# Summing most of a modulation matvec on VectorE instead of TensorE in a hybrid GLA / SSD / PEER block

## The chip, the cores and the metric

One core of one Trainium2 chip runs the kernel. The metric is device time in microseconds, from a run without the profiler; the kernel before was timed three times. One further execution was recorded by the profiler, and all rows below come from that one.

## The reference

One layer over 256 latent tokens with a prefix of 256 context tokens, D = 2048, all float32. Cut to what matters here:

```python
mod_x = jnp.split((silu(c)     @ w_ada + b_ada)[:, None, :],    6, axis=-1)   # w_ada: 2048 x 12288
mod_c = jnp.split((silu(c_ctx) @ w_ada + b_ada)[None, None, :], 6, axis=-1)
hc = rmsnorm(ctx, norm1_w) * (1 + mod_c[1]) + mod_c[0]
hx = rmsnorm(x, norm1_w)   * (1 + mod_x[1]) + mod_x[0]
core_c, ctx_states = branch_core(hc, 1, p, None)        # h @ w_in, GLA and SSD scans
core_x, _          = branch_core(hx, rows, p, ctx_states)
x   = x + mod_x[2] * branch_out(core_x, p)
hx2 = rmsnorm(x, norm2_w) * (1 + mod_x[4]) + mod_x[3]
x   = x + mod_x[5] * peer(hx2, peer_wq, peer_keys, peer_u, peer_v)
return rmsnorm(x, final_norm_w)
```

The change is about the first two lines: a row vector of 2048 numbers times a weight of 96 MB (2048 x 12288 float32), for two vectors, `c` and `c_ctx`. Parts one and two (columns 0 to 4095) are needed for both vectors before anything else can start. Parts three to six are needed later, and with one layer only for `c`.

## The kernel before, in words

Every big weight passes through the class `Stream`: a plan lists 512 KB chunks of 128 x 1024 float32 in the order of use, `_load` (line 39) issues the DMA of a chunk on SP's queue, and `_split` (line 47) turns a float32 chunk into two reduced-precision halves, `hi` with a copy on ScalarE (line 52) and `lo` with a subtraction on VectorE (line 53). A product is then three matmuls per k-tile, hi x hi, hi x lo, lo x hi (`mm3`, lines 314 to 316; `v_part`, lines 322 to 324). `ahead()` keeps loads 7 chunks and splits 3 chunks ahead of use; 4 buffers hold raw chunks and 4 each hold `hi` and `lo`.

The order on each engine is the order in which the Python code issues the instructions. Every engine executes its own list in that order, and SP's list holds the weight loads.

The program goes through these stages.

- **The start.** The tokens `xc` (4 MB) are loaded, `norm1` (lines 279 to 294) squares them on ScalarE (line 284), adds on VectorE (286), sums over partitions on TensorE (287), takes the reciprocal root (289, 290) and multiplies (293). In parallel `ada_piece` (line 248) computes parts one and two of the modulation: `w_ada` chunks of 4 k-tiles x 256 columns, each as four plain float32 matmuls that put a k-tile each into one of four 32-column strips of the array (line 253, `cS` stationary). After four chunks `ada_out` (line 256) copies the partial sums to SBUF (259), transposes them on TensorE (264) and sums them on VectorE (270, 271). The list `START` (line 139) fixes how chunks of the modulation, the modulated tokens `h_pair` (298 to 307) and the first projections are interleaved: each of its ten rounds uses two k-tiles of the first `v` projection and of the small `ld` projection; rounds 0 to 7 also take eight modulation chunks each, and four rounds take one `k` tile.
- **The projections**, with the GLA and SSD scans as generators in the background. `ftile` calls `tick()` after each chunk (lines 895 to 898), and `tick` (342) lets every background generator go one step. Every second tick it calls `ride_piece` (349): one chunk of parts three to six, 2 k-tiles x 512 columns, again four float32 matmuls on line 253. There are 120 such chunks; their loads lie in the same plan, one after every two weight chunks.
- **The output projections** (`oproj`, lines 1044 to 1074), then `w_o` (1101 to 1121). The last 8 modulation chunks were loaded by POOL's queue into `fill` and are multiplied at line 1122, while the second norm is computed.
- **PEER**: queries, routing, then the products with `u` and `v` (lines 1308 to 1479).

```python
def tick(riding=True):
    step()
    ticks += 1
    if riding and ticks % RIDE == 0 and ride_n < 128 - FILL:
        ride_piece()
```

Of the kernel before, what the change touches and what calls it, by code (L numbers as in the profile page):

```python
# [10 lines left out]
F32 = mybir.dt.float32  # L11
# [17 lines left out]
class Stream:  # L29
# [3 lines left out]
    def __init__(self, nc, pool, loads, splits):  # L33
        self.nc, self.pool, self.loads, self.splits = nc, pool, loads, splits
        self.plan, self.raw, self.done = [], {}, {}
        self.cur = self.nd = self.ns = 0
        self.limit = self.side = None

    def _load(self, i):
# [4 lines left out]
        self.nc.sync.dma_start(t, self.plan[i][0])  # L44
        self.raw[i] = t

    def _split(self, i):
        t = self.raw.pop(i)
        if self.plan[i][1]:
            hi = self.pool.tile([P, 1024], F32R, name="hi", tag="hi", bufs=self.splits + 1)  # L50
            lo = self.pool.tile([P, 1024], F32R, name="lo", tag="lo", bufs=self.splits + 1)
            self.nc.scalar.activation(hi, t, AF.Copy)  # L52
            self.nc.vector.tensor_sub(lo, t, hi.bitcast(F32))  # L53
            self.done[i] = (hi, lo)
        else:
            self.done[i] = t
# [25 lines left out]
def hybrid_block_kernel(ctx, tc, A, out):  # L82
# [8 lines left out]
    st = Stream(nc, streams, 7, 3)  # L91
# [13 lines left out]
    def f_chunks(arr, f):  # L105
        return [(arr[f, h], True) for h in range(arr.shape[1])]
# [5 lines left out]
    RIDE, FILL = 2, 8  # L112
# [10 lines left out]
    def v_chunks(hd, q):  # L123
        return [(A["w_v"][hd, 2 * q + i], True) for i in range(2)]

    def unit_chunks(u):
        k, a, b = u
        first, n = {"k": (K0 + 2 * a + b, 1), "q": (Q0 + 2 * a, 2), "r": (R0 + 4 * a, 4), "xs": (X0 + 4 * a + b, 1),
                    "B": (B0 + a, 1), "C": (C0 + a, 1), "z": (Z0 + 4 * a + 2 * b, 2), "gl": (G0 + 2 * a, 2),
                    "v": (0, 0)}[k]  # L130
        if k == "v":
            return sum((v_chunks(a, q) for q in range(4)), [])
        if k == "k" and a < 2:
            return [(W[first, 1], True)]
        return sum((f_chunks(W, first + i) for i in range(n)), [])
# [16 lines left out]
    plan = []  # L152
    for k, a, b in START:
        if k == "ada":
            plan.append((A["w_ada0"][a, b], False))
        elif k == "v" and b == 0:
            plan.append((A["w_v"][0, a], True))
        elif k == "ld" and b == 0 and a % 2 == 0:
            plan.append((A["w_ld"][a // 2], True))
        elif k == "k":  # L160
            plan.append((W[K0 + a, 0], True))
    st.limit = len(plan)
    ride = [(A["w_ada1"][b, i], False) for b in range(16) for i in range(8)]
    nt = 0
    for u in units:
        for c in unit_chunks(u):
            plan.append(c)
            nt += 1
            if nt % RIDE == 0 and len(ride) > FILL:
                plan.append(ride.pop(0))  # L170
    assert len(ride) == FILL
# [6 lines left out]
    last_ada = ride  # L178
    QORD = [(j, e, h) for h in range(2) for j in range(2) for e in range(2)]
    QORD += [(j, e, h) for j in range(2, 8) for e in range(2) for h in range(2)]  # L180
    plan += [(A["w_q"][2 * j + e, h], True) for j, e, h in QORD]
    NB = 32
    for b in range(NB + BACK):
        for i in range(4):
            if b < NB:
                plan += f_chunks(A["u"], 4 * b + i)
            if b >= BACK:
                plan += [(A["v"][b - BACK, 2 * i + j], True) for j in range(2)]
# [3 lines left out]
    xpool = ctx.enter_context(tc.tile_pool(name="hpool", bufs=1))  # L192
# [13 lines left out]
    st.side = (xp, 5)  # L206
# [4 lines left out]
    nc.vector.tensor_scalar(ident, jp, 0.0, None, op0=OP.is_equal)  # L211
    ones = consts.tile([P, P], F32, name="ones")
    nc.vector.memset(ones, 1.0)
    ones512 = consts.tile([P, 256], F32, name="ones512")
    nc.vector.memset(ones512, 1.0)
# [7 lines left out]
    selF = consts.tile([P, 2, P], U32, name="selF")  # L223
    selB = consts.tile([P, 2, P], U32, name="selB")
    for n in range(2):
        nc.vector.tensor_scalar(selF[:, n], jp, 0.0, None, op0=OP.is_ge)
        nc.vector.tensor_scalar(selB[:, n], jp, 0.0, None, op0=OP.is_le)
# [20 lines left out]
    def ada_piece(i, ps, halves, raw=None):  # L248

        raw = (st.get() if raw is None else raw).rearrange("p (g n) -> p g n", g=4)  # L250
        nk = 4 // halves
# [4 lines left out]
    def ada_out(b, ps, halves):  # L256

        sb = xpool.tile([P, 256], F32, name="adasb", tag="adasb", bufs=2)
        nc.scalar.activation(sb, ps, AF.Copy)
        yield  # L260
        yield
        p2 = scbank((P, 2, P))
        for t in range(2):
            nc.tensor.transpose(p2[:, t], sb[:, t * P:(t + 1) * P], ident)
        yield
        p2 = p2.rearrange("p t (j h m) -> p h t m j", h=halves, m=32)
        for h in range(halves):
            n = 2 * (halves * b + h)
            dst = mods[:, :, n:n + 2]
            nc.vector.tensor_reduce(dst.rearrange("p m t -> p t m"), p2[:, h, :, 0:2, :], axis=AX.X, op=OP.add)  # L270
            nc.vector.tensor_add(dst, dst, b_ada[:, None, n:n + 2].to_broadcast([P, 2, 2]))
        ended.add(("ada", b))
        yield
# [57 lines left out]
    ride_n, ride_ps = 0, None  # L331
# [17 lines left out]
    def ride_piece(raw=None):  # L349
        nonlocal ride_n, ride_ps  # L350
        b, i = divmod(ride_n, 8)
        if i == 0:
            ride_ps = adb[:, b % 2]
        ada_piece(i, ride_ps, 2, raw)
        if i == 7:
            bg.insert(0, ada_out(8 + b, ride_ps, 2))
        ride_n += 1

# [5 lines left out]
    adb = psum.tile([P, 2, 256], F32, name="ad")  # L364
    pv0 = [mmbank() for _ in range(4)]
    n1 = norm1()
    plr = pdt = None
    Kt = {a: w4.tile([P, 2, 512], F32, name="s4", tag="s4", bufs=5) for a in range(2)}
    for k, a, b in START:
        if k == "ada":  # L370
            if b == 0:
                ps = adb[:, a // 8]
            ada_piece(b, ps, 1)
            if b == 3:
                bg.append(ada_out(a, ps, 1))
# [28 lines left out]
    st.ahead()  # L404
    SZ = {"s1": 256, "s2": 512, "s4": 1024}
# [37 lines left out]
    def decay(hd):  # L443
# [10 lines left out]
        def one(d, k):  # L454
# [12 lines left out]
            for n in range(2):  # L467
                s = slice(n * P, n * P + P) if d == 0 else slice(n * P + P - 1, n * P - 1 if n else None, -1)
                nc.vector.tensor_tensor_scan(B[:, k, s], ones512[:, :P], mn[:, s], 0.0, op0=OP.mult, op1=OP.add)
# [4 lines left out]
            nc.vector.tensor_tensor_scan(B[:, k, o], ones512[:, :255], mn[:, s], 0.0, op0=OP.mult, op1=OP.add)  # L474
# [152 lines left out]
    def dt_stage(pd):  # L627
# [26 lines left out]
        for c in range(4):  # L654
            s = slice(c * P, c * P + P)
            r = slice(c * P + P - 1, c * P - 1 if c else None, -1)
            nc.vector.tensor_tensor_scan(cum[rows[0], s], ones512[rows[0], :P], dA[rows[0], s], 0.0, op0=OP.mult, op1=OP.add)
            nc.vector.tensor_tensor_scan(cum[rows[1], r], ones512[rows[1], :P], dA[rows[1], r], 0.0, op0=OP.mult, op1=OP.add)
# [419 lines left out]
    def wo_load(i):  # L1078

        if i < 8:  # L1080
            nc.gpsimd.dma_start(x1[:, 2 * i:2 * i + 2], A["xc"][:, 2 * i:2 * i + 2, 0:256])
            if i < FILL:
                fill.append(x1p.tile([P, 1024], F32, name="fill", tag="fill", bufs=FILL))
                nc.gpsimd.dma_start(fill[-1], last_ada[i][0])
# [37 lines left out]
    for t in fill:  # L1122
        ride_piece(t)
# [183 lines left out]

    pq = {}
# [174 lines left out]
def _layouts(I):  # L1483
# [6 lines left out]
    L["w_ada0"] = f(w[:, :2 * D].reshape(4, 4, P, 16, 256).transpose(3, 0, 2, 1, 4)).reshape(16, 4, P, 1024)  # L1490
    L["w_ada1"] = f(w[:, 2 * D:].reshape(8, 2, P, 16, 512).transpose(3, 0, 2, 1, 4)).reshape(16, 8, P, 1024)
# [52 lines left out]
```

## Time and profile before

| what | value |
|---|---|
| median of 3 runs | 3682.08 us (3681.17 to 3683.45) |
| the profiled execution | 3680.64 us, span 3678.8 us |
| TensorE matmul busy | 3619.1 us, 98% of the span |
| TensorE weight load busy | 3194.6 us, 87% |
| VectorE busy | 2227.3 us, 61% |
| ScalarE busy | 1669.3 us, 45% |
| GpSimd busy | 370.1 us, 10% |
| weight DMAs on SP's queue | 625.03 MB, 50.9% of 16 engines |

Busy time of TensorE is modelled: matmuls overlap in the array, and what one costs is read from the distance between the starts of its neighbours. The chain of waits follows the work that ended last back to the start of the program and says which engine held it. A wait in the list of waits is put down to what came last. A number of the profile is a line of the kernel before.

### The profile page before, as it was taken

Reading aid. Unit: us, or ns where it says so; the run is one execution under the profiler, and the core shown is the slowest. Engines: PE = TensorE matmul, PEld = TensorE weight load, DVE = VectorE, ACT = ScalarE, POOL = GpSimd, SP = SyncE. Lnnn points to the kernel's source line nnn. Section 1 sums busy time; section 2 is a strip of 40 time slices with the busy share of each in tenths; the row PEclk is TensorE's granted clock in tenths of the full one; section 3 lists DMA queues with packets and bytes.
Section 4 is the critical chain, followed back from the end, with each engine's and each line's share of the span. In section 5 each row is a group of like instructions: output and inputs, shape, how many; then the busy total and the mean of one; then the engine's idle time right before and its main releaser. Section 6 shows DMA issues by size and latency. Waiting matters only on the chain.

```text
span 3678.8 us, 60850 instructions
## 1 busy us (share of the span) xinstructions
PE 3619.1 (98%) x24799; PEld 3194.6 (87%) x24799; DVE 2227.3 (61%) x3405; ACT 1669.3 (45%) x2248; POOL 370.1 (10%) x424
## 2 busy tenths in 40 slices
PE   6999999999999999999999999999999999999998
PEld 3688888888888888899999999999999999998886
DVE  4364443565566566656555788785555555556777
ACT  3244443344544455555444445554444444444444
POOL 0000000000000000011002006362000000000004
PEclk9999999999999999999999999999999999999999
DMA  8564444546555564467657556677665666666764
GB/s 341 214 177 142 151 166 164 188 152 199 192 172 164 185 204 144 135 206 266 195 189 258 176 179 197 200 200 228 197 198 196 199 197 198 196 199 202 244 227 141
DMA packets 196873, 715.51 MB, mean 194 GB/s; under 512 B 22769, under 2 KB 22913, under 8 KB 196081
## 3 DMA queue, kind: packets, MB, share of 16 engines
q1 hardware_dynamic: 171648, 625.03, 50.9%
q0 software_dynamic: 24944, 86.59, 8.5%
q8 instruction: 195, 3.19, 0.4%
q14 instruction: 86, 0.70, 0.1%
HBM read 679.93 MB, written 31.60 MB: 193 GB/s over the span
## 4 chain that ended last, share of the span: by engine, by line
PE 94%; DVE 2%; DMA 1%; ACT 1%; issue 1%; SPq 0%; POOL 0%; DVEq 0%; ACTq 0%; POOLq 0%
PE mm L314 20%; PE mm L315 20%; PE mm L316 20%; PE mm L1459 6%; PE mm L1460 6%; PE mm L1461 6%; PE ad L253 2%; PE mm L322 2%; PE sc L838 2%; PE mm L323 2%; PE mm L324 2%; PE sc L1267 2%; DVE lo L53 1%; PE sc L579 1%; PE sc L771 1%
## 5 line engine op out<-in xcount | busy, mean ns | idle before, releaser
L53 DVE TENSOR_TENSOR lo<-raw,hi 128x1024 fp32r<-128x1024 f32 x996 | 1235.1, 1247 | 1044.2 <-ACT hi L52 1040.4
L52 ACT ACTIVATE hi<-raw 128x1024 fp32r<-128x1024 f32 x996 | 1048.2, 1058 | 1248.8 <-PE mm L315 549.6
L314 PE MATMUL mm<-Hhi,hi 128*128 128x256 f32 (+1 forms) x2272 | 741.9, 327 | 3.7 <-ACT hi L52 3.1
L316 PE MATMUL mm<-Hhi,lo 128*128 128x256 f32 (+1 forms) x2272 | 723.0, 318 | 2.5 <-DVE lo L53 2.5
L315 PE MATMUL mm<-Hlo,hi 128*128 128x256 f32 (+1 forms) x2272 | 722.1, 318 | 0.0
L314 PE MATMUL mm<-h2hi,hi 128*128 128x256 f32 x2304 | 656.9, 285 | 3.3 <-ACT h2hi L1135 3.3
L315 PE MATMUL mm<-h2lo,hi 128*128 128x256 f32 x2304 | 652.4, 283 | 0.2
L316 PE MATMUL mm<-h2hi,lo 128*128 128x256 f32 x2304 | 651.8, 283 | 0.0
L314 PEld LDWEIGHTS mm<-Hhi,hi 128*128 128x128 f32 x2272 | 433.0, 191 | 82.3 <-issue 45.8
L316 PEld LDWEIGHTS mm<-Hhi,lo 128*128 128x128 f32 x2272 | 433.5, 191 | 33.0 <-DVE lo L53 3.1
L315 PEld LDWEIGHTS mm<-Hlo,hi 128*128 128x128 f32 x2272 | 433.7, 191 | 28.0 <-issue 0.5
L314 PEld LDWEIGHTS mm<-h2hi,hi 128*128 128x128 f32 x2304 | 441.6, 192 | 7.0 <-ACT h2hi L1135 3.7
L315 PEld LDWEIGHTS mm<-h2lo,hi 128*128 128x128 f32 x2304 | 441.9, 192 | 3.9 <-DVE h2lo L1138 0.7
L316 PEld LDWEIGHTS mm<-h2hi,lo 128*128 128x128 f32 x2304 | 441.6, 192 | 0.0
L1460 PE MATMUL mm<-lo,ph 128*128 128x512 f32 x1024 | 405.6, 396 | 4.5 <-DVE lo L53 4.5
L1459 PE MATMUL mm<-hi,ph 128*128 128x512 f32 x1024 | 406.3, 397 | 0.0
L1461 PE MATMUL mm<-hi,pl 128*128 128x512 f32 x1024 | 404.9, 395 | 0.0
L1460 PEld LDWEIGHTS mm<-lo,ph 128*128 128x128 f32 x1024 | 192.7, 188 | 48.6 <-DVE lo L53 6.0
L1461 PEld LDWEIGHTS mm<-hi,pl 128*128 128x128 f32 x1024 | 192.7, 188 | 46.6
L1459 PEld LDWEIGHTS mm<-hi,ph 128*128 128x128 f32 x1024 | 193.0, 188 | 43.1
L698 DVE SCALAR_TENSOR_TENSOR s<-mm,convw,s 128x189 f32<-128x189 f32 (+2 forms) x384 | 160.1, 427 | 111.5 <-ACT s L690 107.5
L316 PE MATMUL mm<-yh,lo 128*128 128x256 f32 x768 | 217.5, 283 | 1.3 <-DVE lo L53 1.3
(328 smaller groups left out, 4518.1 us busy)
## 6 DMA issues: line engine op xcount, KB each, us to landing
raw<-in_w_f_dram SPq DMA_DIRECT2D x288, 512.0 KB, 3.7
raw<-in_u_dram SPq DMA_DIRECT2D x256, 512.0 KB, 3.5
raw<-in_v_dram SPq DMA_DIRECT2D x256, 512.0 KB, 4.2
raw<-in_w_ada_dram SPq DMA_DIRECT2D x184, 512.0 KB, 4.3
raw<-in_w_so_dram SPq DMA_DIRECT2D x64, 512.0 KB, 3.4
raw<-in_w_v_dram SPq DMA_DIRECT2D x32, 512.0 KB, 3.9
s<-cum_d POOLq DMA_DIRECT2D x64, 256.0 KB, 6.6
raw<-in_w_ga_dram SPq DMA_DIRECT2D x32, 512.0 KB, 4.8
```

The lines of the kernel that those rows point to most:

```text
L52: self.nc.scalar.activation(hi, t, AF.Copy)
L53: self.nc.vector.tensor_sub(lo, t, hi.bitcast(F32))
L253: mm_(ps[32 * g:32 * g + 32, :], cS[:, nk * i + g // halves, :], raw[:, g, :], start=i == 0, stop=i == KT // nk - 1, tile_position=(0, 32 ...
L314: mm_(ps, Whi[:, j, :], hi[:, k, tok], start=start and j == 0, stop=False)
L315: mm_(ps, Whi[:, j, :], lo[:, k, tok], start=False, stop=False)
L316: mm_(ps, Wlo[:, j, :], hi[:, k, tok], start=False, stop=stop and j == n - 1)
L322: mm_(pv[tb], Hhi[:, k, tok], Whi[:, j, :], start=k == 0, stop=False)
L323: mm_(pv[tb], Hhi[:, k, tok], Wlo[:, j, :], start=False, stop=False)
L698: nc.vector.scalar_tensor_tensor(dst, xi[:, r0 + dr:r1 + dr, c0 + dc:c1 + dc], w[:, t:t + 1], dst, op0=OP.mult, op1=OP.add)
L1459: mm_(ps[t, i], ghi, Whi, start=j == 0 and k == 0, stop=False)
L1460: mm_(ps[t, i], ghi, Wlo, start=False, stop=False)
L1461: mm_(ps[t, i], glo, Whi, start=False, stop=j == 1 and k == 1)
```

## The change: what it does, and the diff

Parts one and two stay on TensorE, and so do the last 512 columns of part six. Their chunks become pairs of 512 KB loads of 2 k-tiles x 512 columns; four matmuls of 512 columns replace four of 256, so the start has 32 pieces where there were 64, and eight `ada_out` where there were 16. Instead of a transpose, a product with a 0/1 matrix `sel2` brings a result over partitions.

The other 7680 columns of parts three to six, for `c` only, are cut into 15 blocks of 512 columns with 16 k-tiles each, 240 tiles of 128 x 512 (256 KB). At every tick `ride_piece` takes one such tile and VectorE multiplies it by the k-tile's 128 numbers (one per partition) and adds the previous sum: a `tensor_scalar` for the first k-tile of a block, a `scalar_tensor_tensor` for the other 15. After the sixteenth, `ride_out` sums over partitions with four matmuls on TensorE (the sums are stationary, one column of ones moves) and VectorE adds the bias.

These loads leave the plan. `board()` issues them on SP's queue, in the start up to 7 ahead into other pools, later up to 3 ahead into four 256 KB buffers. The weight stream keeps 6 chunks ahead instead of 7, with 3 raw buffers instead of 4. All of its entries are now split, so the first three chunks are split at the place of the first `ahead()`.

```diff
     def _load(self, i):
-        if self.side and not self.plan[i][1] and i % 3:
-            t = self.side[0].tile([P, 1024], F32, name="raw0", tag="raw0", bufs=self.side[1])
-        else:
-            t = self.pool.tile([P, 1024], F32, name="raw", tag="raw", bufs=self.loads - self.splits)
+        t = self.pool.tile([P, 1024], F32, name="raw", tag="raw", bufs=self.loads - self.splits)
...
+    def board(self):
+
+        n = 2 if self.side else 1
+        while self.nr < len(self.rides) and len(self.aboard) + n <= (7 if self.side else 3):
+            for _ in range(n):
+                if not self.side:
+                    t = self.pool.tile([P, 512], F32, name="ride", tag="ride", bufs=4)
+                elif self.nr % 7 > 1:
+                    t = self.side[0].tile([P, 1024], F32, name="raw0", tag="raw0", bufs=5)
+                else:
+                    t = self.side[1].tile([P, 1024], F32, name="s4", tag="s4", bufs=5)
+                self.nc.sync.dma_start(t, self.rides[self.nr])
+                self.aboard.append(t)
+                self.nr += 1
...
-    st = Stream(nc, streams, 7, 3)
+    st = Stream(nc, streams, 6, 3)
...
-    RIDE, FILL = 2, 8
+    FILL = 4
...
-            if c < 8:
-                START.append(("ada", (8 + c, c)[i // 4], i % 4))
+            if c < 8 and i % 2:
+                START.append(("ada", c, i // 2))
...
-    st.side = (xp, 5)
+    st.side = (xp, w4)
+    st.board()
     st.ahead()
...
-    def ada_piece(i, ps, halves, raw=None):
+    adb = psum.tile([P, 512], F32, name="ad")
+
+    def ada_piece(i, raws=None):
...
         for g in range(4):
-            mm_(ps[32 * g:32 * g + 32, :], cS[:, nk * i + g // halves, :], raw[:, g, :], start=i == 0, stop=i == KT // nk - 1,
+            mm_(adb[32 * g:32 * g + 32, :], cS[:, 4 * i + g, :], raws[g // 2][:, g % 2, :], start=i == 0, stop=i == 3,
                 tile_position=(0, 32 * g), skip_group_check=True)
...
+        p2 = scbank((P, 4, 2))
+        for t in range(4):
+            mm_(p2[:, t], sb[:, t * P:(t + 1) * P], sel2, start=True, stop=True)
...
         ticks += 1
-        if riding and ticks % RIDE == 0 and ride_n < 128 - FILL:
+        st.board()
+        if riding and st.aboard and ride_n < 240:
             ride_piece()
...
+        b, k = divmod(ride_n, KT)
+        t = st.aboard.popleft()
+        if k == 0:
+            nc.vector.tensor_scalar(t, t, cS[:, k, 0:1], None, op0=OP.mult)
+        else:
+            nc.vector.scalar_tensor_tensor(t, t, cS[:, k, 0:1], ride_sum, op0=OP.mult, op1=OP.add)
+        ride_sum = t
...
+    def ride_out(b, sums):
+
+        n, t = 32 + 4 * b, 4
+        yield
+        p2 = scbank((P, t))
+        for j in range(t):
+            mm_(p2[:, j:j + 1], sums[:, j * P:(j + 1) * P], ones[:, 0:1], start=True, stop=True)
+        yield
+        nc.vector.tensor_add(mods[:, 0, n:n + t], p2, b_ada[:, n:n + t])
+        yield
```

The rest of the diff drops two constant tiles (broadcast views take their place) and changes the host's layout of `w_ada`.

ScalarE at the head of the program before (`cS` is the activated conditioning vector that every modulation matmul needs, `sq` are the squares of the first norm):

```order
1 L244 ACT_TABLE_LOAD
2 L244 ACTIVATE cS<-cc 128x16x2
3 L245 ACT_TABLE_LOAD
4 L284 ACTIVATE sq_168<-xc 128x512
5 L284 ACTIVATE sq_169<-xc 128x512 x3
```

And with the change:

```order
1 L49 ACT_TABLE_LOAD
2 L49 ACTIVATE hi<-raw 128x1024 x3
3 L251 ACT_TABLE_LOAD
4 L251 ACTIVATE cS<-cc 128x16x2
5 L252 ACT_TABLE_LOAD
6 L294 ACTIVATE sq_183<-xc 128x512
7 L294 ACTIVATE sq_184<-xc 128x512 x3
```

Three splits of weight chunks now stand ahead of `cS` and of the norm; VectorE's list likewise begins with the three `lo` of those chunks, ahead of its constants.

VectorE early in the projections, before (the rows between two `lo` are what one tick gives it):

```order
101 L53 TENSOR_TENSOR lo<-raw,hi 128x1024
102 L642 TENSOR_SCALAR s_1343<-s_1342 128x512
103 L644 SCALAR_TENSOR_TENSOR s_1343<-s_1343,s_1342 128x512 x3
104 L922 TENSOR_TENSOR s_159<-s_159,mm 128x512
105 L53 TENSOR_TENSOR lo<-raw,hi 128x1024
```

The same rows with the change:

```order
71 L50 TENSOR_TENSOR lo<-raw,hi 128x1024
72 L670 TENSOR_SCALAR s_1166<-s_1165 128x512
73 L672 SCALAR_TENSOR_TENSOR s_1166<-s_1166,s_1165 128x512 x3
74 L950 TENSOR_TENSOR s_172<-s_172,mm 128x512
75 L368 SCALAR_TENSOR_TENSOR ride<-ride,cS 128x512
76 L50 TENSOR_TENSOR lo<-raw,hi 128x1024
```

One multiply-add of a tile has been added ahead of the next `lo`, and so it is at each of 240 ticks.

## Rows read from the trace of the kernel before

**Rows 1.** The page: the chain that ended last, shares of the span by engine.
```profile
PE 94%; DVE 2%; DMA 1%; ACT 1%; issue 1%; SPq 0%; POOL 0%; DVEq 0%; ACTq 0%; POOLq 0%
```

**Rows 2.** Busy time by engine in the projections: stretch, length, engines, granted clock, DMA.
```profile
187.00:1400.00 1213.00, 1207.88 (x8029) 1006.40 (x8022) 670.28 (x1145) 560.36 (x943) 52.99 (x82) 1.00 0.53 173
```

**Rows 3.** TensorE's timeline around one riding chunk: start, duration, line, tiles, count.
```profile
602.45 0.28 PE L315 MATMUL mm<-Hlo,hi 128*128 128x256 f32 x1
602.57 0.28 PE L316 MATMUL mm<-Hhi,lo 128*128 128x256 f32 x1
602.78 0.64 PE L253 MATMUL ad<-raw,cS 128*32 128x256 f32 x8
603.35 0.50 PE L314 MATMUL mm<-Hhi,hi 128*128 128x512 f32 x1
```

**Rows 4.** Groups of instructions, whole program: busy time, mean ns, idle time before.
```profile
L644 DVE SCALAR_TENSOR_TENSOR s<-s,s 128x512 f32<-128x512 f32 x8 | 5.5, 690 | 0.2
...
L53 DVE TENSOR_TENSOR lo<-raw,hi 128x1024 fp32r<-128x1024 f32 x996 | 1235.1, 1247 | 1044.2 <-ACT hi L52 1040.4 <-PE sc L548 3.0
L52 ACT ACTIVATE hi<-raw 128x1024 fp32r<-128x1024 f32 x996 | 1048.2, 1058 | 1248.8 <-PE mm L315 549.6 <-PE mm L1461 317.9 <-DMA raw<-in_w_f_dram 194.3
```

**Rows 5.** TensorE's timeline in the routing: four float32 matmuls of 128 columns.
```profile
2240.89 1.06 PE L1267 MATMUL sc<-o,o 128*128 128x128 f32 x8
2241.70 0.36 PE L314 MATMUL mm<-h2hi,hi 128*128 128x256 f32 x1
```

**Rows 6.** TensorE's timeline in the projections: the transposes of one `ada_out`.
```profile
262.99 0.38 PE L264 MATMUL sc<-ident,adasb 128*128 128x128 f32 x2
263.13 0.36 PE L314 MATMUL mm<-Hhi,hi 128*128 128x256 f32 x1
```

**Rows 7.** Busy time in the first 30 us; the last number is GB/s moved.
```profile
0.00:10.00 10.00, 0.00 (x0) 0.00 (x0) 2.06 (x11) 2.98 (x4) 6.66 (x17) 1.00 0.83 311
10.00:20.00 10.00, 2.58 (x10) 0.73 (x10) 4.16 (x6) 4.62 (x8) 0.84 (x2) 1.00 0.89 351
20.00:30.00 10.00, 6.38 (x31) 1.62 (x30) 4.15 (x6) 5.09 (x9) 0.00 (x0) 1.00 0.94 374
```

**Rows 8.** The timelines of ScalarE, VectorE and TensorE in the start.
```profile
8.27 0.23 ACT L244 ACTIVATE cS<-cc 128x32 f32<-128x32 f32 x1
9.81 1.15 ACT L284 ACTIVATE sq<-xc 128x512 f32<-128x512 f32 x2
20.54 1.15 ACT L284 ACTIVATE sq<-xc 128x512 f32<-128x512 f32 x2 [2.64 <-PE sc L287]
...
32.03 3.50 DVE L293 TENSOR_TENSOR xc<-xc,rs 128x1024 f32<-128x1024 f32 x3 [2.68 <-ACT rs L290]
41.69 0.15 DVE L298 SCALAR_TENSOR_TENSOR s<-mods,nw 128x4 f32<-128x4 f32 x1
...
46.74 0.79 PE L322 MATMUL mm<-hi,Hhi 128*128 128x512 f32 x1
```

**Rows 9.** TensorE's timeline in one later round of the start: its back-to-back modulation chunks.
```profile
59.84 1.93 PE L253 MATMUL ad<-raw,cS 128*32 128x256 f32 x32
62.91 0.50 PE L322 MATMUL mm<-hi,Hhi 128*128 128x512 f32 x1
```

**Rows 10.** VectorE alone, busy time in 10 us stretches; the second number after the stretch.
```profile
210.00:220.00 10.00, 9.84 (x23) 1.00 0.67 73
...
1060.00:1070.00 10.00, 9.57 (x18) 1.00 0.46 155
1070.00:1080.00 10.00, 5.30 (x8) 1.00 0.76 249
```

**Rows 11.** Waits of VectorE from 187 to 1400 us: total, times, longest.
```profile
DVE lo L53 <- ACT hi L52: 345.4, 148, 6.4
```

**Rows 12.** DMA issues late in the program: count, KB each, median us to landing.
```profile
raw<-in_v_dram SPq DMA_DIRECT2D x208, 512.0 KB, 4.2
...
yr<-y_d POOLq DMA_DIRECT2D x8, 512.0 KB, 7.1
```

More of the change, by code (lines that the diff above doesn't have):

```diff
@@ L48, in _split, with alight @@
         t = self.raw.pop(i)
[L49 to L56, printed above, removed]
+        hi = self.pool.tile([P, 1024], F32R, name="hi", tag="hi", bufs=self.splits + 1)
+        lo = self.pool.tile([P, 1024], F32R, name="lo", tag="lo", bufs=self.splits + 1)
+        self.nc.scalar.activation(hi, t, AF.Copy)
+        self.nc.vector.tensor_sub(lo, t, hi.bitcast(F32))
+        self.done[i] = (hi, lo)
+    def board(self):
[11 more added lines that the diff above has]
+                self.nr += 1
+    def alight(self):
+        return [self.aboard.popleft() for _ in range(2)]
     def ahead(self):
@@ L105, in f_chunks @@
     def f_chunks(arr, f):
-        return [(arr[f, h], True) for h in range(arr.shape[1])]
+        return [arr[f, h] for h in range(arr.shape[1])]
     W = A["w_f"]
     Q0, K0, R0, Z0, X0, B0, C0, G0 = 0, 8, 16, 32, 64, 96, 104, 112
-    RIDE, FILL = 2, 8
+    FILL = 4
     units = [("k", 0, 0), ("k", 0, 1), ("q", 0, 0)]
@@ L123, in v_chunks @@
     def v_chunks(hd, q):
-        return [(A["w_v"][hd, 2 * q + i], True) for i in range(2)]
+        return [A["w_v"][hd, 2 * q + i] for i in range(2)]
     def unit_chunks(u):
@@ L133, in unit_chunks @@
         if k == "k" and a < 2:
-            return [(W[first, 1], True)]
+            return [W[first, 1]]
         return sum((f_chunks(W, first + i) for i in range(n)), [])
@@ L154, in hybrid_block_kernel @@
         if k == "ada":
-            plan.append((A["w_ada0"][a, b], False))
+            st.rides += [A["w_ada0"][a, 2 * b + i] for i in range(2)]
         elif k == "v" and b == 0:
-            plan.append((A["w_v"][0, a], True))
+            plan.append(A["w_v"][0, a])
         elif k == "ld" and b == 0 and a % 2 == 0:
-            plan.append((A["w_ld"][a // 2], True))
+            plan.append(A["w_ld"][a // 2])
         elif k == "k":
-            plan.append((W[K0 + a, 0], True))
+            plan.append(W[K0 + a, 0])
     st.limit = len(plan)
-    ride = [(A["w_ada1"][b, i], False) for b in range(16) for i in range(8)]
-    nt = 0
+    ride = [A["w_ada1"][b, i] for b in range(15) for i in range(16)]
+    start_rides = len(st.rides)
+    st.rides += ride
     for u in units:
[L166 to L171, printed above, removed]
+        plan += unit_chunks(u)
+    assert len(plan) - st.limit >= len(ride)
     for f in range(16):
@@ L177, in hybrid_block_kernel @@
         plan += f_chunks(A["w_o"], f)
-    last_ada = ride
+    last_ada = [A["w_ada2"][i] for i in range(2 * FILL)]
     QORD = [(j, e, h) for h in range(2) for j in range(2) for e in range(2)]
     QORD += [(j, e, h) for j in range(2, 8) for e in range(2) for h in range(2)]
-    plan += [(A["w_q"][2 * j + e, h], True) for j, e, h in QORD]
+    plan += [A["w_q"][2 * j + e, h] for j, e, h in QORD]
     NB = 32
@@ L187, in hybrid_block_kernel @@
             if b >= BACK:
-                plan += [(A["v"][b - BACK, 2 * i + j], True) for j in range(2)]
+                plan += [A["v"][b - BACK, 2 * i + j] for j in range(2)]
     st.plan = plan
-    xpool = ctx.enter_context(tc.tile_pool(name="hpool", bufs=1))
     es_h = ExitStack()
@@ L222, in hybrid_block_kernel @@
     nc.vector.tensor_scalar(maskB, jp, 0.0, None, op0=OP.is_le)
[L223 to L227, printed above, removed]
+    selF, selB = (m.bitcast(U32)[:, None, :].to_broadcast([P, 2, P]) for m in (maskF, maskB))
     b_ada = cload("b_ada", [P, 96])
@@ L1121, in hybrid_block_kernel @@
     stats(*prev)
-    for t in fill:
-        ride_piece(t)
+    for i in range(FILL):
+        ada_piece(i, fill[2 * i:2 * i + 2])
+    bg.insert(0, ada_out(23))
     rs2 = x1p.tile([P, 256], F32, name="rs2")
```

79 lines of the change are left out of this document (39 added, 40 removed).

## The prediction
> **What bounds the kernel now.** I read the chain of waits first, because a busy share says nothing about what sets the end: TensorE holds 94% of it [rows 1], so a microsecond taken from TensorE's list is a microsecond off the time, as long as nothing else moves into the gap. Then the table of stages: in the projections, 1213 us long, TensorE is busy for 1207.88 us, VectorE for 670.28 (55%), ScalarE for 560 (46%), DMA for 0.53 [rows 2]. The reader is to see that nothing is near TensorE on average. Averages hide crowded stretches, so VectorE is read again in 10 us pieces: 9.84 us of 10 at 210 to 220, 9.57 at 1060 to 1070, 5.30 right behind [rows 10]. Last comes the start, where TensorE waits for the norm and for data [rows 7, 8].
>
> **What it removes.** 120 riding chunks leave TensorE. Around one, the last ordinary matmul starts at 602.57, where the usual distance is 0.12 us (602.45 to 602.57), and the next one starts at 603.35. The chunk therefore costs 0.78 - 0.12 = 0.66 us [rows 3], and 120 of them 79 us, all on TensorE's path. With them go the transposes of their 15 results, 0.14 us each [rows 6], 2 us.
>
> **What it adds on TensorE.** 15 `ride_out` of four matmuls, float32, a fresh 128x128 stationary operand each and one moving column. No row shows one column. The nearest are four float32 matmuls of 128 columns with fresh stationary operands, which hold the engine from 2240.89 to 2241.70, 0.81 us [rows 5]; that is the upper end. The lower end is the pair of transposes, 0.14 us [rows 6]. I take the upper end, since the weight loads are the same in number and size: 15 x 0.81 = 12 us, with 2 us as the lower end. The Trainium skill, "TensorE: Matmul & The Clock Gate", section "Back-to-back issue gap", puts a matmul of 1 to 64 columns at about 60 cycles, 25 ns; eight passes would then be 0.2 us, an estimate from that page, and the sum 9 us lower. I stay with the row, because it contains the weight loads and no run here shows them vanish.
>
> The last 512 columns keep their arithmetic in four larger pieces and still stand where TensorE waits for the second norm; I cost them at nothing. If that cover were gone they would cost what eight chunks cost now, no more.
>
> **What it adds on VectorE.** 240 tiles, 225 of them a multiply-add of 128x512 in SBUF. The same form takes 0.690 us [rows 4]; I use it for the 15 plain multiplications too: 166 us. The stage gets 836 us of VectorE work in about 1140, 73%. So most of it lies beside TensorE. Two places are not covered:
> - Behind the start VectorE is already full [rows 10], and some six to ten of its ticks lie there. Their 4 to 7 us push back what TensorE waits for. I take 6, between 0 (if the waiting stages have slack) and 10.
> - In the crowded piece of each SSD group about 2.3 ticks fall into 10 us: 9.57 + 1.6 = 11.2 us of work. 1.2 us spill into the next piece, which has 4.7 us free. I take 0.5 us for each of eight groups, 4 us, between 0 and 15.
>
> **What it moves in the start.** Three splits now stand ahead of `cS` and the squares on ScalarE, and ahead of the constants on VectorE. They need the chunks that SP issues after `xc` and six modulation loads: 4.2 + 3.1 + 1.6 = 8.9 MB. At 311, 351 and 374 GB/s [rows 7] 6.6 MB are in after 20 us and 8.9 after 26. One `hi` and one `lo` later (1.06 and 1.25 us [rows 4]) it is 28.4; the constants of VectorE, `cS` among them, take some 2 us more, and from the activation of `cS` to the first square it is 1.5 us [rows 8]: the first square starts at about 32 instead of 9.81. From there to the first multiplication with the root it was 22.2 us, 2.6 of them a wait for TensorE [rows 8], which by then has its data: 52. All eight multiplications (1.17 us each, 3.50 for three [rows 8]) now precede `h_pair`: 61. From `h_pair`'s first step to the first `v` matmul it was 5.05 us [rows 8], partly a wait for ScalarE that goes; with 3 the first `v` starts at 64 instead of 46.74, 17 us late. What ScalarE's row shows is that it stands still at a square for 2.64 us for TensorE's sake [rows 8]; whether something behind could have passed, that row cannot say. The Trainium skill, "TensorE: Matmul & The Clock Gate", section "Specifications", calls the queues of ScalarE and VectorE strict first-in-first-out; by that rule the 17 us come, without it none of them.
>
> Some comes back. A round's five chunks back to back held TensorE from 59.84 to 62.91 [rows 9], and three stand alone at 0.66: 5.0 us. Four double pieces stream the same columns with half the changeovers: 4 x (2 x 0.43 + 0.2) = 4.2, where 0.43 is a quarter of the 1.93 us less its tail [rows 9]. With 0.8 us for the new product in place of two transposes of 0.14 and a wait of 0.56 at the bank that goes, I put the gain at 0.5 us in each of six rounds, 3 us. The start ends 14 us later; between 0 and 20.
>
> **Loads.** One raw buffer fewer. A chunk is loaded when the `lo` three chunks earlier ends; landing 4.2 us [rows 12], `hi` 1.06, `lo` 1.25 [rows 4]: 6.5 us for three chunks, 2.2 each, while TensorE takes 24 x 0.12 = 2.9 us [rows 3]. Covered; I allow 2 us, between 0 and 10. In the projections the weights no longer queue on SP behind modulation chunks whose buffers TensorE frees, which can only help.
>
> **The sum.** -79 - 2 + 12 + 6 + 4 + 14 + 2 = -43 us. The profiled execution took 3680.64, so 3638; the median of the runs shown is 1.4 us above it, which is nothing here.
>
> **The rivals.**
> - **VectorE becomes the bound of the projections.** For it: it waits in order, and 345.4 us of its idle time there are waits for `hi` [rows 11]. If these stay, it needs 670 + 166 + 345 = 1181 us, where TensorE needs some 1140 to 1150. Against it: part of these waits is slack that an added instruction simply fills, and `hi` now comes from a stream without modulation chunks in it. Time: about 31 us worse, 3669.
> - **The start costs nothing**, because the splits finish early or the squares don't wait: 3624, and near 3606 with the other terms at their favourable ends.
> - **Slower: three raw buffers don't hide the landing.** The place is everything behind the projections, some 740 chunks. The point from which it decides is a landing of 6.3 us, where (landing + 2.3) / 3 reaches 2.9 us. Loads of the same size on POOL's queue land in 7.1 us [rows 12]; at that each chunk takes 3.15, 0.27 more, 200 us in all: 3840. Against it: the raw loads themselves land in 4.2.
> - **The matmuls were not what held TensorE.** It then waits at the same places for data or a scan, and 3680 stays. Against it: no wait of size stands in the stage, 1207.88 of 1213 us are busy [rows 2].
>
> **How the numbers follow.** The forecast gets 0.62, VectorE as the bound 0.17, the undisturbed start 0.10, the raw buffers 0.06, no effect 0.05. A difference under 0.2%, 7 us, cannot be told from none. Faster: 0.62 + 0.17 + 0.10 = 0.89; the same: 0.05; slower: 0.06. The range goes from 3606, the undisturbed start, to 3670, VectorE as the bound, and leaves out the last two.
>
> **What would show it.** The projections should be some 65 us shorter, with no modulation matmul in them, VectorE near 73% there, the multiply-add near 0.69 us and `ride_out` near 0.8. The first square should start at about 32 us and the first `v` matmul at about 64. Wrong would be: waits of TensorE for VectorE of more than some 20 us in the projections; a first square near 10 us; waits of TensorE for `lo` or `hi` behind the projections; or a multiply-add well over 0.7 us.

## The result, and the profile after

The changed kernel takes 3641.66 us (median of 4 runs, 3637.3 to 3644.84), the kernel before 3681.62 on the same chip: a ratio of 0.989, 95% interval 0.9873 to 0.9907. Forecast were 3638, in a range of 3606 to 3670. The profiled execution spans 3641.1 us, 37.7 less than the one before, and its chain of waits, by engine, reads:

```profile
PE 90%; DVE 5%; DMA 3%; ACT 1%; issue 1%; SPq 0%; POOL 0%; DVEq 0%; ACTq 0%; POOLq 0%
```

Against [rows 1], TensorE has lost 4 points of the chain, VectorE and the DMAs have gained 5. The projections (to compare with [rows 2]) and the groups of VectorE there:

```profile
187.00:1380.00 1193.00, 1175.67 (x7471) 1039.86 (x7470) 847.50 (x1389) 582.44 (x968) 54.08 (x84) 0.99 0.56 180
```
```profile
L50 DVE TENSOR_TENSOR lo<-raw,hi 128x1024 fp32r<-128x1024 f32 x249 | 305.4, 1227 | 256.7 <-ACT hi L49 256.3
L368 DVE SCALAR_TENSOR_TENSOR ride<-ride,cS 128x512 f32<-128x512 f32 x225 | 169.8, 755 | 7.9 <-DMA ride<-in_w_ada_dram 7.6
```

VectorE is busy for 847.50 of 1193 us, 71%. Its wait for `hi` has shrunk from 345.4 us [rows 11] to 256.3: a good part of the added work fills time in which VectorE stood idle. From 300 us on, up to the end of the projections, TensorE waits for VectorE at one kind of place only, three `ride_out` (the view of waits, TensorE, 300 to 1380 us: total, times, longest):

```profile
PE sc L380 <- DVE ride L368: 1.4, 3, 0.5
```

One `ride_out` on TensorE's timeline:

```profile
377.00 0.28 PE L325 MATMUL mm<-Hlo,hi 128*128 128x256 f32 x1
377.12 0.28 PE L326 MATMUL mm<-Hhi,lo 128*128 128x256 f32 x1
377.24 0.95 PE L380 MATMUL sc<-ones,ride 128*128 128x1 f32 x8
378.05 0.36 PE L324 MATMUL mm<-Hhi,hi 128*128 128x256 f32 x1
```

From 377.12 to 378.05 it is 0.93 us, less the usual 0.12: 0.81, although only one column moves. The start, ScalarE first, then VectorE, then TensorE:

```profile
24.68 1.06 ACT L49 ACTIVATE hi<-raw 128x1024 fp32r<-128x1024 f32 x1 [22.67 <-DMA raw<-in_w_v_dram]
...
30.86 0.23 ACT L251 ACTIVATE cS<-cc 128x32 f32<-128x32 f32 x1 [1.29 <-DVE cS L250]
31.11 1.28 ACT L252 ACT_TABLE_LOAD   x1
32.40 1.15 ACT L294 ACTIVATE sq<-xc 128x512 f32<-128x512 f32 x2
```
```profile
53.08 9.18 DVE L303 TENSOR_TENSOR xc<-xc,rs 128x1024 f32<-128x1024 f32 x8 [3.54 <-ACT rs L300]
```
```profile
64.02 0.50 PE L332 MATMUL mm<-hi,Hhi 128*128 128x512 f32 x1 [0.91 <-ACT Hhi L315]
```

ScalarE stands for 22.67 us at the first split; the squares, whose data has long been there, begin at 32.40, and the first `v` matmul at 64.02 instead of 46.74 [rows 8].

**Where the time went.** Of each three products of a split weight take the first: both kernels run the same 6944 of these, here called ordinary matmuls, in the same order, so the start of the n-th in one can be set against the n-th in the other. The table is worked out so from the two traces:

| up to ordinary matmul | stretch | its start before, us | after, us | difference | change |
|---|---|---|---|---|---|
| 0 | norm, first column | 46.74 | 64.02 | +17.3 | +17.3 |
| 24 | two rounds of the start | 77.20 | 100.36 | +23.2 | +5.9 |
| 140 | rest of the start | 183.85 | 207.14 | +23.3 | +0.1 |
| 300 | behind the start | 279.45 | 307.59 | +28.1 | +4.9 |
| 2040 | riding (109 pieces left out, 13 outs) | 1379.64 | 1334.76 | -44.9 | -73.0 |
| 3400 | routes of the outputs | 1958.53 | 1912.18 | -46.4 | -1.5 |
| 3800 | `w_o`, second norm | 2119.70 | 2081.91 | -37.8 | +8.6 |
| 6943 | the rest | 3668.77 | 3631.16 | -37.6 | +0.2 |

So three losses, 23 + 5 + 9 us, stand against one gain. A second trace of the changed kernel (**again**, below) differs from the first by 1.5 us in the row behind the start, by 2.1 in the `w_o` row and by at most 1.0 in the others; single steps of that size say nothing. The second loss of the start has its row on SP's queue, and TensorE's stretch beside it:

```profile
76.35 1.97 SPq L64 DMA_DIRECT2D raw<-in_w_ada_dram  x4
78.37 0.92 SPq L64 DMA_DIRECT2D s<-in_w_ada_dram  x2
91.22 0.33 SPq L42 DMA_DIRECT2D raw<-in_w_ld_dram  x1
91.65 2.29 SPq L64 DMA_DIRECT2D raw<-in_w_ada_dram  x5
```
```profile
90.00:100.00 10.00, 4.96 (x22) 1.31 (x21) 4.15 (x9) 1.26 (x2) 0.00 (x0) 0.87 0.76 286
```

SP issues nothing between 79.3 and 91.2 us; then a weight load goes out, and right behind it five modulation loads. TensorE is busy for half of the following stretch, and its granted clock falls to 0.87 there.

### The profile page after: what moved, and what is told of

Same layout as the page of the kernel before. It is cut to its first block, busy times and chain, and to the rows that moved or that the text cites. A ratio compares the mean times of both kernels' runs of the same rounds, so it can differ in the third digit from the quotient of the medians.

```text
span 3641.1 us, 58912 instructions
## 1 busy us (share of the span) xinstructions
PE 3546.8 (97%) x23679; PEld 3182.4 (87%) x23679; DVE 2369.1 (65%) x3569; ACT 1667.7 (46%) x2226; POOL 369.9 (10%) x424
## 4 chain that ended last, share of the span: by engine, by line
PE 90%; DVE 5%; DMA 3%; ACT 1%; issue 1%; SPq 0%; POOL 0%; DVEq 0%; ACTq 0%; POOLq 0%
PE mm L324 19%; PE mm L326 19%; PE mm L325 19%; PE mm L1490 6%; PE mm L1489 6%; PE mm L1491 6%; PE mm L332 2%; PE sc L1296 2%; PE mm L334 2%; PE mm L333 2%; DVE lo L50 1%; PE sc L866 1%; PE sc L607 1%; PE sc L799 1%; DMA x_d<-x 1%
## 5 line engine op out<-in xcount | busy, mean ns | idle before, releaser
L324 PE MATMUL mm<-yh,hi 128*128 128x256 f32 x768 | 216.9, 282 | 0.7 <-ACT hi L49 0.7
```

Of the source, the lines that this page charges most:

```text
L324: mm_(ps, Whi[:, j, :], hi[:, k, tok], start=start and j == 0, stop=False)
```

## The experiments

All edits are to the changed kernel unless said otherwise. The changed kernel itself was timed again beside the first three of them: **again**.

> The changed kernel once more, for comparison with the three beside it on the same chip: 3641 us as before, within 4 us (its runs so far lie between 3637 and 3645), 0.989 of the kernel before.

Measured: 3642.41 us (3639.85 to 3643.1), 0.9892 (0.9876 to 0.9909).

**The start: ScalarE's order.**

The first call only loads; the splits come with a second call, in the start's loop behind `ada_piece(b)`.

```diff
-    st.ahead()
+    st.ahead(False)
...
+            if (a, b) == (0, 3):
+                st.ahead()
```

> The first three splits are issued after the first column's four ada pieces instead of ahead of everything; their loads stay where they are. Theory (the start is late because ScalarE runs its instructions in order, and Silu of c and the squares of the norm now stand behind splits that wait for the seventh to ninth load): the first square begins at 12 to 20 us instead of 32.4, the first matmul of v at 46 to 51 us instead of 64.0, and the whole kernel takes 14 to 18 us less, 3623 to 3628 us. Rival (the start is bound by its loads: the pieces of the ada columns and x fill the DMA engines, and ScalarE's order only shows where one waits): the first matmul of v moves by less than 5 us and the time stays over 3636 us. Second rival (the start is regained later): v moves to under 51 us, but the following rounds of the start, which wait for the loads of the ada columns, hold it up, so that the end of the start gains under 8 us.

Measured: 3636.93 us (3633.82 to 3640.18), 0.9882 (0.9865 to 0.9898); first `v` matmul at 58.06. Neither the theory nor either rival: 6 us of 17 at the first `v`, 5 us of the time. ScalarE was free, but SP's queue shows what came in its place:

```profile
16.11 0.33 SPq L42 DMA_DIRECT2D raw<-in_w_ld_dram  x1
17.30 20.52 SPq L42 DMA_DIRECT2D raw<-in_w_v_dram  x2
38.63 0.33 SPq L42 DMA_DIRECT2D raw<-in_w_ld_dram  x1
39.77 0.33 SPq L42 DMA_DIRECT2D raw<-in_w_v_dram  x1
40.15 0.42 SPq L64 DMA_DIRECT2D raw<-in_w_ada_dram  x1
```
```profile
30.00:40.00 10.00, 3.89 (x10) 0.70 (x10) 6.45 (x7) 4.16 (x5) 0.00 (x0) 0.67 0.16 43
```

The fourth weight load needs one of three raw buffers, the buffers come free with the splits, and the splits now come late; the modulation loads behind it wait with it, and in the stretch from 30 to 40 us the core moves 43 GB/s. The wait had moved from ScalarE's order to SP's. Three more kernels separate the two.

**start_three_loads**: the same, with `self.cur + 3` in place of `self.cur + self.loads` in the first call.

> start_later with only three weight loads issued ahead of the norm, as many as there are raw buffers, and all on SP's queue. In start_later the third load of v stood 20.5 us on SP's queue with the ada loads behind it. Theory: without that wait the first matmul of v comes at 46 to 50 us, but the later rounds keep their pauses: 10 to 15 us less than the changed kernel, 3626 to 3632 us. Rival (start_later's 6 us are all that ScalarE's order was worth): 3635 us or more.

Measured: 3628.67 us (3627.01 to 3630.1), 0.9853 (0.9838 to 0.9868); first `v` at 51.32, and the second round still 7.6 us longer than in the kernel before. The time and the pause are as the theory had them; the first `v` comes a little behind its 46 to 50.

**start_pool_queue**: the place of the splits is the changed kernel's; the modulation loads of the start leave SP's queue.

```diff
-                self.nc.sync.dma_start(t, self.rides[self.nr])
+                (self.nc.gpsimd if self.side else self.nc.sync).dma_start(t, self.rides[self.nr])
```

> The changed kernel with one edit: the loads of the start's ada chunks are issued on GpSimd's queue, those of the weights stay on SP's. Theory (in the start the two kinds of load share SP's queue, and an ada load stands behind a weight load that waits for a raw buffer; the loads are what bounds the start, so each pause of the queue is paid): the pause at 79 to 91 us goes with the 8 us that it cost, the first weights land before 20 us and with them the splits that stand ahead of the norm on ScalarE, so the first matmul of v comes at 48 to 56 us instead of 64.0, and the kernel takes 12 to 20 us less, 3622 to 3630 us. Rival (the 16 DMA engines are full anyway, another order of issue only shifts which load comes late): under 4 us, over 3637 us.

Measured: 3627.68 us (3626.67 to 3629.19), 0.9852 (0.9837 to 0.9867). The time lies in the theory's range, but not by its way: the round that lost 8 us lost nothing (the 24th ordinary matmul gains 8.9 us on the 12th against the changed kernel), while the first `v` came at 61.39, hardly earlier. The splits did have their first data before 20 us (18.82), but the second and third weight loads still landed at 21 and 24, and ScalarE's order held the squares to 29.00.

**start_later_pool**: both edits.

> The same, and the first splits after the first column's pieces (as in start_later). Theory of two queues' order (ScalarE's and SP's, each in order): the first matmul of v at 46 to 50 us, as in the kernel before, and 16 to 24 us less than the changed kernel, 3618 to 3626 us. Rival (with SP's order mended the place of the splits no longer matters): within 3 us of start_pool_queue.

Measured: 3614.91 us (3613.2 to 3616.47), 0.9817 (0.9803 to 0.983): 27 us less than the changed kernel, more than the theory's 24. First square and first `v` matmul:

```profile
10.32 1.15 ACT L294 ACTIVATE sq<-xc 128x512 f32<-128x512 f32 x2
```
```profile
48.50 0.50 PE L332 MATMUL mm<-hi,Hhi 128*128 128x512 f32 x1
```

This settles the start: two queues that work in order. With the other one mended, ScalarE's is worth 12 to 13 us (3627.68 against 3614.91) and SP's some 22 (3636.93 against 3614.91). The two are not a sum, since either alone still holds up part of what the other frees: both together are worth 27. The move to GpSimd's queue also changes the kind of queue (in the pages of the two kernels 33.6 MB go from hardware_dynamic to software_dynamic), which was not tried apart; but the pause that it removes is SP's own, 79.3 to 91.2 us, and start_three_loads, all on SP's queue, shows ScalarE's share without it. The Trainium skill, "Perfetto Trace Analysis", section "Tensor Engine Instruction (MATMUL, LD_WEIGHTS)", calls the queues of ScalarE, VectorE and GpSimd strictly first in, first out; ScalarE's rows agree, 22.67 us at a split while the squares stood behind it.

**The `w_o` stage.**

The ride buffers have a pool of their own, closed in `open_out`, which now also waits for the last `ride_out`; a fourth raw buffer takes their place.

```diff
+        if self.more and i % 4 == 3:
+            t = self.more.tile([P, 1024], F32, name="raw4", tag="raw4", bufs=1)
...
+        es_r.close()
+        st.more = ctx.enter_context(tc.tile_pool(name="more", bufs=1, side="right"))
+        st.loads = 7
```

> The ride buffers go into a pool of their own, which is closed when the last ride is done, and a fourth raw buffer is opened in its place, so that from the last SSD group on there are seven loads ahead as in the kernel before; start and riding keep three raw buffers. Theory (the w_o stage is 8.6 us longer than in the kernel before because three raw buffers do not hide a load's landing there): 6 to 9 us less, all of them in the w_o stage, where ScalarE's 13 waits for the load (39.9 us idle before the splits) go; 3632 to 3636 us. Rival (the w_o stage is longer for the loads of x and of the last ada chunks, which run on the GpSimd queue, or for the order of the last pieces): the stage stays within 2 us of the changed kernel, 3639 to 3643 us.

Measured: 3635.48 us (3633.59 to 3643.58), 0.988 (0.9864 to 0.9897): 6.2 to 6.9 less than the changed kernel's two medians. On the traces 4.9 us of 8.6 go between the 3400th and the 3800th ordinary matmul, 1.1 are gained in the start, which the edit doesn't touch. ScalarE's waits in the stage, first the changed kernel's (1915 to 2037 us), then this one's (1913 to 2031):

```profile
ACT hi L49 <- DMA raw<-in_w_o_dram: 34.5, 12, 5.4
```
```profile
ACT hi L52 <- PE mm L330: 31.5, 19, 2.5
```

With three raw buffers the split waits for the load, with four for TensorE, as in the kernel before. What TensorE loses by it is its own wait in the stage, first the changed kernel's, then this one's; the kernel before has no such row there:

```profile
PE mm L326 <- DVE lo L50: 4.5, 7, 1.0
```
```profile
PE mm L331 <- DVE lo L53: 1.1, 3, 0.4
```

The four timed runs overlap with the changed kernel's, so the traces have to decide. The same row of the table differs by 4.9 us here, by 7.8 between both (below) and start_later, and by 7.2 between all_four (below) and start_later_pool: the buffer makes 5 to 8 of the 8.6 us. Whether anything besides it is left the traces don't tell, since before_few_pieces (below), which keeps the four buffers, is 3.6 us longer than the kernel before in that row too. Behind the stage, from 2037 us to the end, loads come late as well:

```profile
ACT hi L49 <- DMA raw<-in_v_dram: 67.6, 34, 6.5
```

In the kernel before that wait is 6.7 us in 3 times. But TensorE loses only 0.2 us there. **both** joins this edit and start_later:

> Both edits together. If the two losses are independent, the gains add: 20 to 27 us less than the changed kernel, 3614 to 3622 us, 0.983 of the kernel before. If one of them only moves a wait to the other's place, less than 18 us.

Measured: 3630.44 us (3628.83 to 3632.59), 0.9864 (0.9848 to 0.9881): 11 to 12 less, against 5 + 6 of the two alone. They add; that it is under the 18 us of the second case comes from start_later's share, which was expected too high.

**The price of a riding chunk.** The kernel before, without 90 of its 120 chunks' matmuls:

```diff
-        ada_piece(i, ride_ps, 2, raw)
+        if raw is not None or i in (0, 7):
+            ada_piece(i, ride_ps, 2, raw)
+        else:
+            st.get()
```

> The kernel before, with the matmuls of 90 of its 120 riding chunks left out (the first and the last piece of each block of eight stay; the loads stay too), so parts three to six of the modulation are wrong sums. It measures the prediction's first term by itself. By the price in the prediction, 0.66 us a piece, 59 us less: 3620 to 3625 us. Theory that a piece costs its neighbours time too (the rows of the changed kernel show some 9 us gone beside the pieces over the riding stage): 65 to 72 us less, 3610 to 3617 us. Rival (part of the pieces stood in idle time of TensorE that stays when they go): 35 to 50 us less, over 3631 us.

Measured: 3614.87 us (3612.19 to 3617.72), 0.9815 (0.9802 to 0.9829): 67.6 us less, 0.75 for each chunk. The prediction read 0.66 from [rows 3]. The missing 0.09 stands in the same timeline of the kernel before, one row further:

```profile
603.68 0.39 PE L315 MATMUL mm<-Hlo,hi 128*128 128x512 f32 x1
603.91 0.40 PE L316 MATMUL mm<-Hhi,lo 128*128 128x512 f32 x1
```

The first matmul behind the chunk takes 0.33 us to the next one (603.35 [rows 3] to 603.68), the second 0.23: 0.10 more. In all the 120 places the first takes 0.10 to 0.11 us more than that usual distance. The changeover back is paid by the neighbour, after the point at which the prediction stopped counting.

**VectorE's load.** **no_sums** drops the 225 `scalar_tensor_tensor` (the last tile of a block is multiplied instead), **sums_twice** issues each one twice on the same tile.

> The changed kernel without its 225 scalar_tensor_tensor; the loads, the buffers and the 15 summing matmul groups stay (only the last chunk of a block, scaled, is summed, so parts three to six of the modulation are wrong). It takes 170 us of work from VectorE. Theory (VectorE has room for the sums except where it is crowded behind the start, about 187 to 290 us): 5 to 16 us less, gained before TensorE's 300th ordinary matmul (308 us), and nothing after it; 3626 to 3637 us. Rival (VectorE bounds the riding stage, a little in many places): more than 20 us less, spread over the stage. Third case (the sums lie beside other work everywhere): within 3 us.

Measured: 3640.94 us (3639.98 to 3641.25), 0.9885 (0.987 to 0.99), as the third case has it: 0.7 to 1.5 us. On the trace the theory's 4.9 us before the 300th ordinary matmul are there, with 2 more in three steps of 0.7 up to the 2040th. These three steps stand at 824, 1051 and 1277 us, at the three `ride_out` that wait for the last sum. 5.4 us are given back later, in several places from the 2560th ordinary matmul to the end; by what was not tried, and the 2.4 of them in the `w_o` row are hardly more than the 2.1 by which the two traces of the changed kernel differ there.

> The changed kernel with each of the 225 scalar_tensor_tensor issued twice on the same tile (the second one's sums are wrong): 170 us more on VectorE, which would be busy for 85% of the riding stage instead of 71%. Theory (room left): 5 to 25 us more, most of it in the crowded stretch before 308 us. Rival (VectorE is at its bound, what is added is paid): 80 to 170 us more.

Measured: 3680.01 us (3675.51 to 3685.02), 0.9993 (0.9984 to 1.0002): 38 us more for 170 us of work, between theory and rival. VectorE in the projections:

```profile
187.00:1400.00 1213.00, 1177.04 (x7336) 1036.28 (x7335) 1001.96 (x1594) 574.67 (x954) 54.73 (x84) 0.98 0.55 176
```

The 83% are an average of two stages. VectorE alone (length, busy time) from the 300th to the 1140th ordinary matmul (GLA and the head of the SSD part), and from there to the 2040th (SSD groups); first the changed kernel, then this one:

```profile
308.00:809.00 501.00, 315.98 (x510) 1.00 0.54 173
809.00:1335.00 526.00, 409.69 (x673) 1.00 0.61 197
```
```profile
311.00:813.00 502.00, 385.65 (x606) 1.00 0.53 172
813.00:1367.00 554.00, 489.62 (x782) 0.98 0.59 188
```

In the first stretch VectorE goes from 63% to 77% and nothing is lost. In the second it goes from 78% to 88% and 28.6 us are lost, at seven places (4.4, 3.4, 4.1, 4.4, 3.9, 4.1, 4.4 between the 1140th and the 1980th ordinary matmul): at the last products of five SSD groups (L867) and at the `ride_out` (L381) beside them or between them. TensorE's waits show 17 us of it:

```profile
PE sc L867 <- issue: 10.8, 5, 2.2
PE sc L381 <- DVE ride L369: 6.1, 5, 2.3
```

Behind five of the ten waits the granted clock of TensorE falls: 0.83 in the 10 us that hold one of them, 1.00 ahead of it.

```profile
1060.00:1070.00 10.00, 7.24 (x59) 6.15 (x58) 9.82 (x17) 2.11 (x2) 0.00 (x0) 0.83 0.38 116
```

I read this as the crowded piece in each group, which with single sums still fits but for the three waits of `ride_out`; that it is this piece, and not the stage's share, was not tried apart.

**rides_later.**

```diff
-        if riding and st.aboard and ride_n < 240:
+        if riding and ticks > 30 and st.aboard and ride_n < 240:
```

> The changed kernel with the first sum at tick 31 instead of tick 1 (there are 308 ticks for 240 sums), so that VectorE has nothing of the ride while it serves dt_stage and the first keys. Theory (the sums delay dt_stage's operands there): 4 to 14 us less, 3628 to 3638 us, all of it before 308 us, and the end of the ride, 30 ticks later, costs nothing. Rival (what TensorE waits for there is work of VectorE that was there before, uncovered since 12 pieces less stand on TensorE): within 2 us.

Measured: 3637.09 us (3636.21 to 3638.26), 0.9876 (0.9861 to 0.9891): 5 us less, in the theory's range. On the trace 8.0 us are gained between the 140th and the 300th ordinary matmul (6.5 against the trace of again), 3 more than without any sums. But the later end of the ride is not free: 2.1 come back between the 2040th and the 2560th, where two more `ride_out` now stand, and another 4.1 from the 3400th on, by what was not tried. The wait that stands out behind the start, TensorE's longest there in the changed kernel: the same wait in the kernel before, in the changed one and in this one:

```profile
PE sc L683 <- DVE s L672: 1.2, 1, 1.2
```
```profile
PE sc L711 <- DVE s L700: 8.7, 1, 8.7
```
```profile
PE sc L711 <- DVE s L700: 6.2, 1, 6.2
```

The sums are 2.5 of the 7.5 us; the other 5 remain without them (no_sums shows 6.2 as well), so their cause is another. Pieces that no longer cover VectorE's work for dt_stage are a part of it: in before_few_pieces, where two of the three pieces ahead of this wait are left out and no sum is on VectorE, it is

```profile
PE sc L686 <- DVE s L675: 2.8, 1, 2.8
```

That is 1.6 us for two pieces; three, an estimate from it, would make 2.4 of the 5. The rest stays open. The clock goes with the wait. In the changed kernel, where it ends at 243.1 us, the granted clock is 0.62 in the 10 us around its end; in the kernel before no 10 us from 190 to 250 are under 0.91:

```profile
240.00:250.00 10.00, 6.92 (x41) 6.95 (x42) 9.84 (x21) 4.41 (x7) 0.54 (x1) 0.62 0.62 92
```

**all_four**: start_later_pool, raw4_late and rides_later in one kernel.

> The four edits together: GpSimd's queue for the start's ada loads, the first splits after the first column, a fourth raw buffer from the last SSD group on, the first sum at tick 31. If the gains are independent, they add to those measured singly against the changed kernel's 3642: 27 (start_later_pool), 6 to 7 (raw4_late) and 5 (rides_later), so 3601 to 3608 us, 0.979 of the kernel before. If rides_later's gain was part of the start's disorder, or is given back at the end of the ride as part of it was, 3607 to 3612 us. Over 3612 us the gains are not independent.

Measured: 3599.07 us (3598.32 to 3601.45), 0.9779 (0.9766 to 0.9793). That is 2 us under the range for independent gains. The kernel before is faster here too (3680.06), so the fair sum goes by the distance to the kernel before beside each run: 40.0 us for the change, 27.6, 6.6 and 5.8 more for the three edits alone, together 80; measured are 81. The gains are independent.

## Why the prediction was right, and where its terms were not

The mechanism came out as forecast: the chunks left TensorE, VectorE took their work without binding, and the start paid. That the time was only 3.7 us off is partly luck: single terms were further off and cancelled, with more gain in the pieces and more loss around them.

- **Chunks off TensorE, -79.** Mis-sized: 0.75 each, not 0.66 (before_few_pieces), so -90. The step that failed is "the next one starts at 603.35. The chunk therefore costs 0.78 - 0.12": it counted to the next matmul's start and not through its changeover. In the riding stretch 109 chunks x 0.75, 13 pairs of transposes (2.3) and 13 outs (10.8) make -73.3, measured -73.0: nothing else of size happens there.
- **`ride_out`, +12.** Right: 0.81 each; three of them waited 1.4 us together for the last sum, and lost 0.7 each by it. Four matmuls of one column with fresh stationary operands hold TensorE as long as four of 128 columns did [rows 5]. The Trainium skill, "TensorE: Matmul & The Clock Gate", section "Back-to-back issue gap", gives the 25 ns for 1 to 64 columns as the gap of an isolated matmul and says that this has no budget for the weight load. The trace agrees with that reservation: eight records with fresh weights take 0.81 us, 0.10 each, so the prediction's estimate of 0.2 us from the 25 ns had no place here.
- **VectorE.** The multiply-add takes 0.755 us, not 0.690: 170 us, and 71% of the stage against 73 forecast. That VectorE doesn't bind was right, and why the rival fell is seen in the wait for `hi`: 89 us of its idle time were slack. The forecast of 4 us for the SSD groups was 2, and came another way: what no_sums gains there are the three waits of `ride_out`, 0.7 each. The work that spills over into the next piece of a group, which the prediction priced at 0.5 us a group, cost TensorE nothing that the traces show.
- **Behind the start, +6.** Mis-sized: the stretch from the 140th to the 300th ordinary matmul is 4.9 us longer, but it lost ten chunks (7.5) and got one out (0.8), so the loss itself is 4.9 + 7.5 - 0.8 = 11.6. Without the sums 4.9 of it go (no_sums; 3.3 against the trace of again), with the sums put off 8.0 (rides_later; 6.5). The prediction's step named the sums alone. The pieces that no longer cover VectorE's work are a second part, and the granted clock of 0.62 around the end of the long wait a third; their shares were not measured apart, and part of the loss stays open.
- **The start, +14.** The chain that the prediction followed came out within 1.5 us (first square 32.40 for 32, `h_pair` 62.37 for 61, first `v` 64.02 for 64). Mis-sized was the way back: "I put the gain at 0.5 us in each of six rounds". The rounds lost 6 us, since modulation loads wait on SP behind weight loads for raw buffers. So +23 instead of +14. The prediction saw that the weights no longer queue behind modulation chunks in the projections; in the start it's the other way round, and it didn't look there.
- **One raw buffer fewer, +2.** Mis-sized: the `w_o` stage lost 8.6, the buffer 5 to 8 of them (raw4_late, both, all_four). The step "covered", 6.5 us for three chunks against 2.9 each, takes the usual landing of 4.2 us; in this stage ScalarE waited up to 5.4 us for one. The slower rival named the right mechanism; its price of 200 us needed TensorE to wait at every later chunk. Late chunks there were outside this stage too (67.6 us of ScalarE's waits for `v` alone), but TensorE lost 0.2 us there: a split that comes late is not yet a matmul that waits.

Taken together: -90 - 2 + 12 from the riding itself, 23 + 12 + 9 in losses around it, -1 elsewhere: -37, where the forecast had -43.

## What to carry to other kernels

Price a piece by taking some of them out, or count through the instruction behind it: a changeover is paid on both sides. When loads of two kinds share a queue, draw for each one what buffer it waits for and what stands behind it; an edit that frees one engine's order can hand the wait to a DMA queue's, and here only mending both paid in full (27 us against 5 and 14). Work can be given to an engine at 55% of a stage, but read its share stage by stage: 77% cost nothing in one here, 88% cost 28.6 us in another. Where a stretch is crowded, put the work off past it if there are ticks to spare (rides_later, 5 us).

## What the runs showed that was not expected

- A float32 matmul of one moving column, with a fresh 128x128 stationary operand, costs as much as one of 128 columns: 0.81 us for four in both cases.
- The same `scalar_tensor_tensor` form, 128x512 in SBUF, took 0.690 us in eight cases of one place [rows 4] and 0.737 to 1.227 (median 0.744) in 225 of another. What makes the difference was not tried.
- Doubling the sums, 170 us on an engine that was 71% busy, cost 38 us, nearly all of it in the SSD groups and behind the start: most of an engine's idle time could be filled, but not the last of it.
- A wait of TensorE can come with a lower clock behind it: in the 10 us around the end of the 8.7 us wait in the changed kernel the granted clock was 0.62, and in sums_twice it fell behind five of the ten waits of the SSD groups.
